# FFN2's last product: one activation table for the final norm, matmuls of a token tile ahead of the scalings, the last bank in halves, weight splits ahead of token sums

## The chip, the core and the metric

The kernel runs on one core of a Trainium2 chip. Its engines are TensorE (PE, with its weight loads shown as PEld), VectorE (DVE), ScalarE (ACT), GpSimd (POOL) and SyncE (SP). Each works through its own list of instructions in order, and they wait for each other by semaphores. The metric is the device time of one execution in microseconds, as the median of repeated runs.

## What is computed

The reference is one layer of a streaming encoder: a half-step feed-forward network (FFN1), two token mixers side by side, a second feed-forward network (FFN2), and a norm at the end. The change is in the last part:

```python
x = x + 0.5 * swiglu(rms_norm(x, ffn2_norm[l]), ffn2_w1[l], ffn2_w3[l], ffn2_w2[l])
return rms_norm(x, final_norm)

def swiglu(h, w1, w3, w2):
    return (jax.nn.silu(h @ w1) * (h @ w3)) @ w2
```

There are 512 tokens and 1024 columns, all in float32. The product of concern is the last one, `hidden @ w2`, with 22 blocks of 128 hidden rows, followed by the residual sum and the final norm of each token.

## The kernel before

**Three matmuls for one.** A float32 operand is split into a high part (rounded to the fast float32 form, a cast on ACT) and a low part (the rest, a subtraction on DVE). A product is high x high, high x low and low x high.

**Seven products for eight.** `ByTokens.run` multiplies hidden rows 0 to 15 with `w2` by a Strassen-like scheme: both operands are cut in two each way, sums of the quarters are made, and seven products of quarters take the place of eight. Rows 16 to 21 are multiplied plainly. Results are kept by tokens in eight banks X, Y, Z, W, two each, of 128 tokens x 512 columns.

- The sums of the **weights** are made by DMA: `onto` (L1893) issues on POOL's queue a DMA that adds a part of `w2` onto a buffer that holds another. The buffers are `chain` (four, tile `raw` in the trace) and `b22` (four, tile `wu`). `fetch` (L1888) loads a part plainly on SP's queue.
- The sums of the **tokens** are made on DVE from the hidden parts, in four units u, by `whole` (L1917: one operation of 1024 columns, two of 512), `s1` (L1925: one of 512 on DVE, then a cast `h0to` on ACT, then, as `rest`, another of 512 on DVE) and `s234` (L1931: three of 512).
- `prep` (L1955) splits a weight buffer: a cast of 1024 columns on ACT (`whi`, L1965) and the rest on DVE (`wlo`, through L1903). It uses three pairs of buffers in turn, so a split waits until PE is done with the piece of three splits earlier. `parts` (L1941) splits token sums in the same way.
- `seventh` (L1975) and `plainly` (L1985) are one **pass** on PE: twelve matmuls of 512 columns with one piece of weights, eight with the high part, then four with the low part. I number the passes from 0 in the order in which PE runs them: 0 to 3 go into X, 4 to 7 into Y (weights `b21`), 8 to 11 are plain passes (weights `f`), 12 to 15 go into Z, 16 to 19 into X (weights `chain` with a part added), 20 to 27 use `b22`, before and after a part is added (24 is the first after it), 28 is plain, 29 to 32 use `chain` with a third part, 33 is plain.
- `snap` (L1995) copies a pair of banks to memory on ACT. `parts`, `prep`, `snap` and all the sums are recorded by `keep`, which holds them in the order of the program text on each engine. That text is written by hand, from L2008 to L2142; it sets the order that the change alters. A DMA with no `keep` may still be moved by the scheduler.

**The end phase** (L2143 to L2174) goes over four token tiles t of 128 tokens. Each tile has two banks c of 512 columns: twelve matmuls for the first, six for the second. DVE reads a bank, scales it by half the token's norm factor and adds the residual (L2156); ACT squares the result and sums it (L2157); a small DVE operation (L2159) adds the epsilon; the reciprocal root is exp(-0.5 ln(.)) on ACT, Ln in L2160 and Exp in L2161; DVE multiplies both halves by it and by the gain `fg` (L2165), and SP stores them (L2166). In the last tile, DVE makes the product with the gain early (L2170), and ACT (L2171) and DVE (L2172) scale one half each. Before Ln and before Exp, the compiler places a load of the activation table that has the function.

Of the kernel before, what the change touches and what calls it, by code (L numbers as in the profile page):

```python
# [18 lines left out]
P = 128  # L19
# [32 lines left out]
def kernel(  # L52
# [401 lines left out]
    class Seven:  # L454
# [59 lines left out]
        def rest(s, dst, src, hi):  # L514
            keep(dve.tensor_tensor(dst, src, f32(hi), op=ALU.subtract))  # L515
# [1336 lines left out]
    class ByTokens:  # L1852
# [26 lines left out]
        def run(s, hh, hl, h, w2, hp):  # L1879
# [8 lines left out]
            def fetch(tag, k0, c):  # L1888
                to = unit(tag)
                keep(nc.sync.dma_start(to, part(k0, c)))  # L1890
                return to

            def onto(to, k0, c):  # L1893
                keep(nc.gpsimd.dma_start(to, part(k0, c), accum_op=ALU.add))
# [2 lines left out]
                return y[:, t // 2, t % 2 * P:(t % 2 + 1) * P] if len(y.shape) == 3 else y[:, t * P:(t + 1) * P]  # L1897

            def mm(ps, a, b, start=False, stop=False):
                keep(pe.matmul(ps[:], a, b, start=start, stop=stop, skip_group_check=True))  # L1900

            def two(to, a, b, op=ALU.subtract):
                keep(dve.tensor_tensor(to, a, b, op=op))  # L1903
# [21 lines left out]
            def s1(u):  # L1925
                v, to = RB[u][:, :, H:T], [h[:, 2 * u:2 * u + 2, i, H:T] for i in range(2)]
                two(v, RA[u][:, :, H:T], v)
                keep(act.copy(to[0], v))
# [20 lines left out]
            def plain_h(k0, t0):  # L1949
                return lambda k, a: [token(y[k0 + k], t0 + a) for y in (hh, hl)]  # L1950
# [4 lines left out]
            def prep(src, own=None):  # L1955
                n = made[0]
                if own:
                    hi, lo = [unit(t, F32R) for t in own]
                else:
                    made[0] += 1  # L1960
                    if n % 3 == 2:
                        hi, lo = fp.tile([P, 2, T], F32R, name="whi", tag="fg")[:], unit("E30", F32R, "wlo")
                    else:
                        hi, lo = [wp.tile([P, 2, T], F32R, tag=t, name=t, bufs=2)[:] for t in ("whi", "wlo")]
                keep(act.copy(hi, src))  # L1965
# [29 lines left out]
            def snap(ps, name, t0):  # L1995
                got = []
                for a in range(2):
                    o = xp.tile([P, T], F32, name=f"{name}{a}", tag=f"x{'hl'[a]}{dict(x0=4, up=5, m5=6)[name]}")[:]
                    keep(act.activation(o, ps[a][:], AF.Copy, scale=sc[:, t0 + a:t0 + a + 1]))
                    got.append(o)  # L2000
                return got
# [18 lines left out]
            seventh(X, plain_h(4, 0))  # L2020
            prep(b21[1])
            rest = s1(1)
            s234(1)
            rest()
            f = [fetch(tags[0], 16, 0)]
            seventh(X, plain_h(6, 0))
            prep(b21[2])
            f.append(fetch(tags[1], 16, 1))
            whole(2)
            seventh(Y, plain_h(K2, 0), True)  # L2030
            prep(b21[3])
            x0 = snap(X, "x0", 0)
            f.append(fetch(tags[2], 18, 0))
            seventh(Y, plain_h(K2 + 2, 0))
            prep(f[0])
            f.append(fetch(tags[3], 18, 1))
            seventh(Y, plain_h(K2 + 4, 0))
            prep(f[1])
            rest = s1(2)
            s234(2)  # L2040
            rest()
            seventh(Y, plain_h(K2 + 6, 0))
            prep(f[2])
            whole(3)
            plainly(16, 0, (0, 1))
            prep(f[3])
            plainly(16, 1, (2, 3), True)
            prep(chain[0])
            onto(chain[0], K2, 1)
            plainly(18, 0, (0, 1))  # L2050
            prep(chain[1])
            onto(chain[1], K2 + 2, 1)
            plainly(18, 1, (2, 3))
            prep(chain[2])
            onto(chain[2], K2 + 4, 1)
            rest = s1(3)
            seventh(Z, plain_h(0, 2), True)
            prep(chain[3])
            onto(chain[3], K2 + 6, 1)
            rest()  # L2060
            s234(3)
# [8 lines left out]
            onto(chain[1], K2 + 2, 0)  # L2070
            seventh(Z, plain_h(6, 2))
            left.append(parts(S2, 2))
            prep(chain[2])
            onto(chain[2], K2 + 4, 0)
# [4 lines left out]
            onto(chain[3], K2 + 6, 0)  # L2079
# [60 lines left out]
            residual(3)  # L2140
            for key in ((20, 0), (20, 1), (18, 0)):
                last[key] = take()  # L2142
            for t in range(NB):  # L2143
                y = ys[t]
                sums_, b_, r = [sc[:, o + t * n:o + (t + 1) * n] for o, n in ((4, 2), (12, 1), (16, 1))]
                first = 1 if t < 2 else 0
                for c in (first, 1 - first):
                    ks = [(k0, *last[k0, c], k) for k0 in (18, 20) if k0 == 20 or c == first for k in range(2)]
                    to = bank_of[t][c]
                    for k0, hi, lo, k in ks:  # L2150
                        mm(to, token(hh[k0 + k], t), hi[:, k])
                        mm(to, token(hl[k0 + k], t), hi[:, k])
                    for k0, hi, lo, k in ks:
                        mm(to, token(hh[k0 + k], t), lo[:, k], stop=(k0, k) == (20, 1))
                    v = y[:, c * T:(c + 1) * T]
                    keep(dve.scalar_tensor_tensor(v, to[:], sc[:, t:t + 1], v, op0=ALU.mult, op1=ALU.add))  # L2156
                    keep(act.activation(tmp("junk")[:], v, AF.Square, accum_out=sums_[:, c:c + 1]))  # L2157
                    if c == first:
                        keep(dve.tensor_scalar(b_, sums_[:, c:c + 1], 1.0 / D, RMS_EPS, op0=ALU.mult, op1=ALU.add))  # L2159
                keep(act.activation(r, sums_[:, 1 - first:2 - first], AF.Ln, bias=b_, scale=1.0 / D))  # L2160
                keep(act.activation(r, r, AF.Exp, scale=-0.5))  # L2161
                for c in range(2):
                    cs = slice(c * T, (c + 1) * T)
                    if t + 1 < NB:
                        keep(dve.scalar_tensor_tensor(y[:, cs], y[:, cs], r, fg[:, cs], op0=ALU.mult, op1=ALU.mult))  # L2165
                        nc.sync.dma_start(out[0, t * P:(t + 1) * P, cs], y[:, cs])  # L2166
                if t + 1 == NB:
                    g = [tmp("yg") for _ in range(2)]
                    for c in range(2):
                        keep(dve.tensor_tensor(g[c][:], y[:, c * T:(c + 1) * T], fg[:, c * T:(c + 1) * T], op=ALU.mult))  # L2170
                    keep(act.activation(g[0][:], g[0][:], AF.Copy, scale=r))  # L2171
                    keep(dve.tensor_scalar(g[1][:], g[1][:], r, None, op0=ALU.mult))  # L2172
                    for c in range(2):
                        nc.sync.dma_start(out[0, t * P:(t + 1) * P, c * T:(c + 1) * T], g[c][:])  # L2174

    tokens = ByTokens()
    ffn(nrm2, ffn2_w1, ffn2_w3, ffn2_w2, None,
# [26 lines left out]
```

## Time and profile before

| what | us |
|---|---|
| median of 3 runs | 1138.43 (1138.19 to 1140.03) |
| the profiled execution, own time | 1137.67 |
| its span on the core | 1136.0 |
| PE busy in the span | 1110.1 |
| DVE busy | 911.3 |
| ACT busy | 657.6 |
| end phase, from the first tile's first matmul to the span's end | 1099.14 to 1136.0 |

The profile is of one execution. A timeline row has the start in us from the span's beginning, the duration in us, the engine, the line of the kernel, the operation, output and inputs by the program's tile names, and shapes; where the engine had been idle, brackets give for how long and which engine's result ended it. L1900 is the helper for matmuls and L1903 the one for DVE's sums and low parts, so such rows are told apart by their tiles. A row with "x2" merges two instructions. Matmuls overlap: one lasts 0.39 us, and the next starts 0.227 us after it.

### The profile page before, as it was taken

What the parts mean: (1) busy time and instruction counts of PE and PEld (TensorE: products, weight loads), DVE (VectorE), ACT (ScalarE), POOL (GpSimd) and SP (SyncE); (2) the same over time, 40 slices, a digit from 0 to 9 for tenths busy, and PEclk for the clock granted to TensorE, in tenths of its full rate; (3) what the DMA queues carried; (4) which work ended last, traced back from release to release, by engine and by line L of the source; (5) the groups of instructions that cost most, each with busy time, mean ns of one, the idle gap of its engine ahead of it and who ended that gap; (6) DMA issues with size and microseconds to landing.
All of it is one profiled execution on the core that took longest, in us unless ns stands there. A gap on an engine that the chain in (4) does not pass through costs nothing. (4 is left out here: it accounts for less than half of the span.)

```text
span 1136.0 us, 19524 instructions
## 1 busy us (share of the span) xinstructions
PE 1110.1 (98%) x7640; PEld 974.5 (86%) x7640; DVE 911.3 (80%) x1427; ACT 657.6 (58%) x1090; POOL 106.3 (9%) x170
## 2 busy tenths in 40 slices
PE   9999999999999999999999999999999999999992
PEld 7899999988887888887777777888999999978782
DVE  6889999977566888677776668779988999989563
ACT  6645665543346755355878767536666566645545
POOL 2000000010000112311000010130000000012200
PEclk9999999999999999999999999999999999999996
DMA  8433333354434434355113236633344333377941
GB/s 260 135 93 107 99 112 106 100 176 121 121 108 112 109 98 116 101 142 139 38 39 110 66 109 205 185 93 93 112 139 121 113 96 109 113 204 162 209 167 74
DMA packets 198074, 139.55 MB, mean 123 GB/s; under 512 B 10558, under 2 KB 178558, under 8 KB 197982
## 3 DMA queue, kind: packets, MB, share of 16 engines
q1 hardware_dynamic: 185710, 110.77, 33.3%
q0 software_dynamic: 10032, 26.74, 9.1%
q8 instruction: 60, 0.98, 0.4%
q10 hardware_dynamic: 2240, 0.79, 0.3%
q14 instruction: 32, 0.26, 0.1%
HBM read 123.41 MB, written 14.88 MB: 122 GB/s over the span
## 5 line engine op out<-in xcount | busy, mean ns | idle before, releaser
L133 ACT CAST whi<-raw 128x1024 fp32r<-128x1024 f32 (+2 forms) x93 | 90.0, 969 | 103.3 <-issue 16.6
L134 DVE TENSOR_TENSOR wlo<-raw,whi 128x1024 fp32r<-128x1024 f32 (+2 forms) x93 | 104.3, 1122 | 22.4 <-ACT whi L133 22.1
L142 PE MATMUL zc<-xh,wlo 128*128 128x256 f32 x296 | 83.7, 283 | 0.0
L142 PE MATMUL zc<-xl,whi 128*128 128x256 f32 x296 | 83.7, 283 | 0.0
L142 PE MATMUL zc<-xh,whi 128*128 128x256 f32 x296 | 83.7, 283 | 0.0
L142 PE MATMUL za<-e,wtwo 128*128 128x256 f32 x480 | 64.2, 283 | 0.0
L142 PEld LDWEIGHTS za<-e,wtwo 128*128 128x128 f32 x480 | 59.6, 188 | 0.0
L512 ACT CAST wtwo<-wsum 128x1024 fp32r<-128x1024 f32 x37 | 38.9, 1052 | 31.1 <-PE za L142 31.1
L142 PEld LDWEIGHTS zc<-xh,wlo 128*128 128x128 f32 x296 | 56.7, 191 | 0.0
L142 PEld LDWEIGHTS zc<-xl,whi 128*128 128x128 f32 x296 | 56.7, 191 | 0.0
L142 PEld LDWEIGHTS zc<-xh,whi 128*128 128x128 f32 x296 | 56.6, 191 | 0.0
L142 PE MATMUL pgt<-xh,whi 128*128 128x512 f32 x128 | 53.0, 414 | 0.0
L515 DVE TENSOR_TENSOR wlo<-raw,whi 128x1024 fp32r<-128x1024 f32 x41 | 49.9, 1218 | 2.5 <-ACT whi L512 2.5
L524 DVE TENSOR_TENSOR wsum<-wsum,raw 128x512 f32<-128x512 f32 x74 | 50.9, 688 | 1.2
L524 DVE TENSOR_TENSOR wsum<-raw 128x512 f32<-128x512 f32 x74 | 50.5, 683 | 0.0
L142 PE MATMUL pgt<-xh,wlo 128*128 128x512 f32 x128 | 50.1, 391 | 0.0
L142 PE MATMUL pgt<-xl,whi 128*128 128x512 f32 x128 | 50.0, 391 | 0.0
L512 ACT CAST whi<-wsum 128x1024 fp32r<-128x1024 f32 x37 | 38.8, 1048 | 16.7 <-PE zc L142 13.4
L512 ACT CAST whi<-raw 128x1024 fp32r<-128x1024 f32 x41 | 43.1, 1051 | 8.9 <-PE zc L142 7.9
L598 ACT ACTIVATE fs<-fa 128x512 f32<-128x512 f32 x39 | 24.7, 633 | 38.8 <-DVE fa L631 31.5
L515 DVE TENSOR_TENSOR wtwo<-wsum,wtwo 128x1024 fp32r<-128x1024 f32 x37 | 45.1, 1218 | 0.0
L515 DVE TENSOR_TENSOR wlo<-wsum,whi 128x1024 fp32r<-128x1024 f32 x37 | 45.0, 1217 | 0.0
(693 smaller groups left out, 3612.4 us busy)
## 6 DMA issues: line engine op xcount, KB each, us to landing
raw<-in_ffn_w_dram SPq DMA_DIRECT2D x106, 512.0 KB
raw<-in_w_in_dram SPq DMA_DIRECT2D x40, 512.0 KB
wu<-in_ffn_w_dram SPq DMA_DIRECT2D x18, 512.0 KB
raw<-in_ffn_w_dram POOLq DMA_DIRECT2D x12, 512.0 KB, 8.8
raw<-in_w_out_dram SPq DMA_DIRECT2D x8, 512.0 KB
raw<-in_ffn_w_dram SPq DMA_DIRECT2D x8, 384.0 KB
gsave<-gs SPq DMA_DIRECT2D x9, 256.0 KB
xin<-in_x_dram SPq DMA_DIRECT2D x4, 512.0 KB
```

The lines of the kernel that those rows point to most:

```text
L133: marks["wide"] = act.copy(hi[:], raw[:])
L134: marks["rest"] = (eng or dve).tensor_tensor(lo[:], raw[:], hi[:].bitcast(F32), op=ALU.subtract)
L142: mm = pe.matmul(ps, w, x_, start=first and n == 0, stop=last and n == 2, skip_group_check=chain)
L512: keep(act.copy(dst, src))
L515: keep(dve.tensor_tensor(dst, src, f32(hi), op=ALU.subtract))
L524: keep(dve.tensor_tensor(to, a, b, op=ALU.add))
L598: keep(act.activation(sa[:], a_[:], AF.Silu))
```

## The change

Four edits, all in `ByTokens.run`:

1. **One table.** `preload_act_table_set("natural_log_exp_and_others")` stands ahead of the end phase.
2. **Scalings later.** The two scalings and stores of a tile become a function `finish(t)`. For tiles 0 and 1 it is called one tile later, after that tile's second bank has been read and squared; for tile 2 it is called between the two banks of tile 3.
3. **The last bank in halves.** Tile 3's second bank is multiplied, read, squared and at the end scaled in two halves of 256 columns; its first half's gain product is made early, the other two pieces are scaled in one operation each. There are three last stores for two.
4. **Weights ahead of sums.** In the hand-written order, `prep` of a pass's weights moves up by about one pass, ahead of `s1` or between `s1` and `s234`, with the fetches that follow it; the four `onto(chain[u], K2 + 2 * u, 0)` move from behind their `prep`s to behind the last `onto` of `b22`.

```diff
             onto(chain[3], 6, 1)
+            prep(b21[0])
             rest = s1(0)
+            seventh(X, plain_h(2, 0))
+            prep(b21[1])
+            f = [fetch(tags[0], 16, 0)]
             s234(0)
             rest()
-            seventh(X, plain_h(2, 0))
-            prep(b21[0])
-            whole(1)
             seventh(X, plain_h(4, 0))
-            prep(b21[1])
+            prep(b21[2])
+            f.append(fetch(tags[1], 16, 1))
+            whole(1)
+            seventh(X, plain_h(6, 0))
+            prep(b21[3])
+            f.append(fetch(tags[2], 18, 0))
             rest = s1(1)
+            x0 = snap(X, "x0", 0)
+            seventh(Y, plain_h(K2, 0), True)
+            prep(f[0])
+            f.append(fetch(tags[3], 18, 1))
             s234(1)
             rest()
...
             prep(chain[0])
-            onto(chain[0], K2, 0)
...
             onto(b22[3], 6, 1)
+            for u in range(NU):
+                onto(chain[u], K2 + 2 * u, 0)
...
+            keep(act.preload_act_table_set("natural_log_exp_and_others"))
+
+            def finish(t):
+                y, r = ys[t], sc[:, 20 + t:21 + t]
+                for c in range(2):
+                    cs = slice(c * T, (c + 1) * T)
+                    keep(dve.scalar_tensor_tensor(y[:, cs], y[:, cs], r, fg[:, cs], op0=ALU.mult, op1=ALU.mult))
+                    nc.sync.dma_start(out[0, t * P:(t + 1) * P, cs], y[:, cs])
...
+                    if t + 1 == NB and c != first:
+                        finish(t - 1)
+                        g = tmp("yg")
+                        keep(dve.tensor_tensor(g[:], y[:, 0:T], fg[:, 0:T], op=ALU.mult))
+                    pieces = [slice(0, T)] if c == first or t + 1 < NB else [slice(0, H), slice(H, T)]
+                    for cols in pieces:
...
+                if 0 < t < NB - 1:
+                    finish(t - 1)
+                keep(act.activation(r, q, AF.Ln, bias=b_, scale=1.0 / D))
                 keep(act.activation(r, r, AF.Exp, scale=-0.5))
...
+            keep(act.activation(g[:], g[:], AF.Copy, scale=r))
+            nc.sync.dma_start(out[0, t * P:(t + 1) * P, 0:T], g[:])
+            for cols in (slice(T, T + H), slice(T + H, D)):
+                keep(dve.scalar_tensor_tensor(y[:, cols], y[:, cols], r, fg[:, cols], op0=ALU.mult, op1=ALU.mult))
+                nc.sync.dma_start(out[0, t * P:(t + 1) * P, cols], y[:, cols])
```

On DVE, where the first unit's token sums stand: `rb<-ra,rb` is `s1`, the rows with `s_` are `s234`, `wlo<-raw` is the low part of pass 3's weights and `wlo<-wu` that of passes 4 and 5.

```order
 L1903 TENSOR_TENSOR rb<-hh_9405,hl_9406 128x512
 L1903 TENSOR_TENSOR wlo<-raw,whi 128x1024
+L1903 TENSOR_TENSOR wlo<-wu,whi 128x1024
 L1903 TENSOR_TENSOR rb<-ra,rb 128x2x256
+L1903 TENSOR_TENSOR wlo<-wu,whi 128x1024
 L1903 TENSOR_TENSOR s_10841<-rb,ra 128x512
 L1903 TENSOR_TENSOR s_10843<-ra 128x512
```

One weights' low part now stands ahead of `s1`, and another between `s1` and `s234`.

On ACT at the same place and on to the second unit: `h0to` is the cast inside `s1`, `x_` are the snaps of X.

```order
 L1965 CAST whi<-raw 128x1024 x2
+L1965 CAST whi<-wu 128x1024
 L1928 CAST h0to_8201<-rb 128x2x256
-L1965 CAST whi<-wu 128x1024 x2
+L1965 CAST whi<-wu 128x1024 x3
 L1928 CAST h0to_8201<-rb 128x2x256
-L1965 CAST whi<-wu 128x1024 x2
-L1999 ACTIVATE x_10976<-tx_10833,small 128x512
-L1999 ACTIVATE x_10978<-tx_10834,small 128x512
```

One of the casts of weights has moved ahead of the first `h0to`; each of the later ones that DVE takes next after an `s1` stands behind that unit's `h0to`.

On DVE in the end phase, from the second token tile's first bank to the fourth's: L2169 is the reading of a bank, L2172 the small operation, L2147 the scaling. This is the order after:

```order
L2169 SCALAR_TENSOR_TENSOR yt<-tz_10838,small,yt 128x512
L2172 TENSOR_SCALAR small<-small 128x1
L2169 SCALAR_TENSOR_TENSOR yt<-ty_10836,small,yt 128x512
L2147 SCALAR_TENSOR_TENSOR yt<-yt,small,fgain 128x512 x2
L2169 SCALAR_TENSOR_TENSOR yt<-tx_10833,small,yt 128x512
L2172 TENSOR_SCALAR small<-small 128x1
L2169 SCALAR_TENSOR_TENSOR yt<-tw_10839,small,yt 128x512
L2147 SCALAR_TENSOR_TENSOR yt<-yt,small,fgain 128x512 x2
L2169 SCALAR_TENSOR_TENSOR yt<-tx_10834,small,yt 128x512
```

Before, the same rows stood there with two scalings behind each tile's second reading; now the scalings behind a tile's second reading are those of the tile before it.

More of the change, by code (lines that the diff above doesn't have):

```diff
@@ L1899, in mm @@
             def mm(ps, a, b, start=False, stop=False):
-                keep(pe.matmul(ps[:], a, b, start=start, stop=stop, skip_group_check=True))
+                keep(pe.matmul(ps if isinstance(ps, bass.AP) else ps[:], a, b, start=start, stop=stop, skip_group_check=True))
             def two(to, a, b, op=ALU.subtract):
@@ L2022, in run @@
+            prep(b21[3])
+            f.append(fetch(tags[2], 18, 0))
             rest = s1(1)
+            x0 = snap(X, "x0", 0)
+            seventh(Y, plain_h(K2, 0), True)
+            prep(f[0])
+            f.append(fetch(tags[3], 18, 1))
             s234(1)
             rest()
[L2025 to L2028, printed above, removed]
+            seventh(Y, plain_h(K2 + 2, 0))
+            prep(f[1])
@@ L2029, in run @@
             whole(2)
[L2030 to L2036, printed above, removed]
             seventh(Y, plain_h(K2 + 4, 0))
-            prep(f[1])
+            prep(f[2])
             rest = s1(2)
+            seventh(Y, plain_h(K2 + 6, 0))
+            prep(f[3])
             s234(2)
             rest()
-            seventh(Y, plain_h(K2 + 6, 0))
@@ L2043, in run @@
-            prep(f[2])
-            whole(3)
             plainly(16, 0, (0, 1))
-            prep(f[3])
-            plainly(16, 1, (2, 3), True)
             prep(chain[0])
             onto(chain[0], K2, 1)
-            plainly(18, 0, (0, 1))
+            whole(3)
+            plainly(16, 1, (2, 3), True)
             prep(chain[1])
             onto(chain[1], K2 + 2, 1)
-            plainly(18, 1, (2, 3))
+            rest = s1(3)
+            plainly(18, 0, (0, 1))
             prep(chain[2])
@@ L2149, in run @@
                     to = bank_of[t][c]
[L2150 to L2174, printed above, removed]
+                    if t + 1 == NB and c != first:
+                        finish(t - 1)
+                        g = tmp("yg")
+                        keep(dve.tensor_tensor(g[:], y[:, 0:T], fg[:, 0:T], op=ALU.mult))
@@ new lines, in run @@
+                    pieces = [slice(0, T)] if c == first or t + 1 < NB else [slice(0, H), slice(H, T)]
+                    for cols in pieces:
+                        for k0, hi, lo, k in ks:
+                            mm(to[:, cols], token(hh[k0 + k], t), hi[:, k, cols])
+                            mm(to[:, cols], token(hl[k0 + k], t), hi[:, k, cols])
+                        for k0, hi, lo, k in ks:
+                            mm(to[:, cols], token(hh[k0 + k], t), lo[:, k, cols], stop=(k0, k) == (20, 1))
+                        v, q = y[:, c * T + cols.start:c * T + cols.stop], sc[:, 4 + 3 * t + n:5 + 3 * t + n]
+                        keep(dve.scalar_tensor_tensor(v, to[:, cols], sc[:, t:t + 1], v, op0=ALU.mult, op1=ALU.add))
+                        keep(act.activation(tmp("junk")[:, cols], v, AF.Square, accum_out=q))
+                        if n == 0:
+                            keep(dve.tensor_scalar(b_, q, 1.0 / D, RMS_EPS, op0=ALU.mult, op1=ALU.add))
+                        elif cols.stop < T:
+                            keep(dve.scalar_tensor_tensor(b_, q, 1.0 / D, b_, op0=ALU.mult, op1=ALU.add))
+                        n += 1
```

17 lines of the change are left out of this document (7 added, 10 removed).

## Prediction

> **What bounds the kernel now.** I read the page first, then its last two windows, then the timelines of PE, ACT, DVE and SP in the end phase, and last those of DVE, ACT and PE where the token sums are made.
>
> ```profile
> PE 1110.1 (98%) x7640; PEld 974.5 (86%) x7640; DVE 911.3 (80%) x1427; ACT 657.6 (58%) x1090; POOL 106.3 (9%) x170
> 1060.00:1100.00 40.00, 38.05 (x168) 31.19 (x167) 24.94 (x27) 19.92 (x23) 3.68 (x4) 1.00 0.79 205
> 1100.00:1137.00 37.00, 15.62 (x69) 12.58 (x68) 14.59 (x25) 18.77 (x33) 0.00 (x0) 0.75 0.15 57
> ```
>
> PE is busy for 98% of the span, so elsewhere only PE's waits can be won. The last window (columns: PE, PEld, DVE, ACT, POOL, granted clock, DMA share, GB/s) is different: PE works 15.6 of 37 us. PE's part of the end phase:
>
> ```profile
> 1099.14 0.39 PE L1900 MATMUL tz<-wu,hh 128*128 128x512 f32 x1
> 1101.86 0.39 PE L1900 MATMUL ty<-whi,xh 128*128 128x512 f32 x1
> 1103.22 0.39 PE L1900 MATMUL tz<-wu,hh 128*128 128x512 f32 x1
> 1115.23 0.39 PE L1900 MATMUL tw<-wlo,hh 128*128 128x512 f32 x1
> ```
>
> Call S = 1099.14 the start of the first token tile. Twelve matmuls take 2.72 us (0.2266 each), a tile's eighteen 4.08, and PE is through at 1115.62, 20.4 us before the span's end at 1136.0. What runs after it is a chain of ACT and DVE:
>
> ```profile
> 1102.69 0.74 DVE L2156 SCALAR_TENSOR_TENSOR yt<-tz,small,yt 128x512 f32<-128x512 f32 x1
> 1104.22 0.15 DVE L2159 TENSOR_SCALAR small<-small 128x1 f32<-128x1 f32 x1 [0.79 <-ACT junk L2157]
> 1104.29 0.74 DVE L2156 SCALAR_TENSOR_TENSOR yt<-ty,small,yt 128x512 f32<-128x512 f32 x1
> 1105.06 0.63 ACT L2157 ACTIVATE junk<-yt 128x512 f32<-128x512 f32 x1 [0.88 <-DVE yt L2156]
> 1105.60 0.19 ACT L2157 ACTIVATION_READ_ACCUMULATOR junk<-yt 128x1 f32 x1
> 1105.80 1.28 ACT L2160 ACT_TABLE_LOAD   x1
> 1107.10 0.29 ACT L2160 ACTIVATE small<-small 128x1 f32<-128x1 f32 x1
> 1107.41 1.28 ACT L2161 ACT_TABLE_LOAD   x1
> 1108.70 0.20 ACT L2161 ACTIVATE small<-small 128x1 f32<-128x1 f32 x1
> 1108.94 1.42 DVE L2165 SCALAR_TENSOR_TENSOR yt<-yt,small,fgain 128x512 f32<-128x512 f32 x2 [3.91 <-ACT small L2161]
> 1110.27 0.75 DVE L2156 SCALAR_TENSOR_TENSOR yt<-tz,small,yt 128x512 f32<-128x512 f32 x1
> 1132.22 0.81 SPq L2174 DMA_DIRECT2D out_dram<-yg  x2
> ```
>
> A tile costs 7.58 us (1102.69 to 1110.27) where PE needs 4.08. DVE waits 3.91 us for the square root's two halves, of which two table loads are 2.56, and the next tile's reading of its bank stands behind that wait. So the end phase is bound by this chain.
>
> **Part one: the end phase.** The loads inside the loop go (eight of 1.28, 10.2 us, all on the chain), and one is placed behind the last weights' cast, hidden by PE's first tile: ACT has nothing to do there until the first Square. Ln starts at 1107.10, 0.02 us after its load ended at 1107.08, so a load's row is its whole price. The Trainium skill (ScalarE: Activation LUTs, "What ACT_TABLE_LOAD costs") puts a switch of sets at 1283 ns and a drain of about 1380 behind it; by that the eight would be worth 21.3 us, 11.1 more than by the row, and the trace has no place for them.
>
> Two scalings (L2165) now stand behind the next tile's two bank readings, so they no longer hold PE's banks' reading up. DVE per middle tile: a reading 0.74, the wait and the small op to the second reading 0.86, that one 0.67, scalings 1.34: 3.6 us, below PE's 4.08. PE therefore becomes the bound of the first three tiles, and the last tile follows PE. From S, in us:
>
> - tile 3's first bank: PE ends at 3 x 4.08 + 2.88 = 15.12; reading to 15.89, Square with its read to 16.65, small op 16.75;
> - then DVE has tile 2's two scalings (1.34, to 18.09) and the early gain product:
>
> ```profile
> 1127.72 1.28 DVE L2170 TENSOR_TENSOR yg<-yt,fgain 128x512 f32<-128x512 f32 x2
> 982.45 0.42 DVE L635 SCALAR_TENSOR_TENSOR fh<-za,fs 128x256 f32<-128x256 f32 x1
> 992.78 0.37 ACT L512 COPY fa<-za 128x256 f32<-128x256 f32 x1
> ```
>
> - product 0.60, to 18.69. The last bank's halves are in by then: PE ends at 16.7, or 18.1 if each 256-column matmul cost as much as a 512-column one; either way before 18.69, so halving costs PE nothing that counts;
> - half a reading, 0.41 by the row with 256 columns, to 19.10; half a Square. No row shows it: between 0.37 (the 256-column copy without a read) and 0.73 (the whole one with its read). I take 0.47, the copy with the part of the read that sticks out (0.10 here). Then small op, second half's reading from 19.70 to 20.11, Square to 20.61, Ln 20.91, Exp 21.14;
> - half a scaling, 0.41, to 21.55; SP issues the first output at 21.6, two more 0.43 behind each other.
>
> Before, SP's first of two issues stood at 1132.22 = S + 33.1, and the span ended 3.8 later. Now 21.6 + 3.8, plus 0.43 for a third issue, minus some 0.35 for a last transfer of half the size: 25.5 against 36.9. Part one is worth -11.4 us. Bounds: halved Squares 0.26 longer each, +0.5; if they and the middle steps run without my gaps, -0.7.
>
> **Part two: weights ahead of the token sums.** A pass is twelve matmuls with one split piece of weights; three buffers hold pieces. Before, DVE is the engine that PE waits for:
>
> ```profile
> 1008.36 1.22 DVE L1903 TENSOR_TENSOR wlo<-raw,whi 128x1024 fp32r<-128x1024 f32 x1
> 1009.50 0.68 DVE L1903 TENSOR_TENSOR rb<-ra,rb 128x512 f32<-128x512 f32 x1
> 1010.22 0.62 ACT L1928 CAST h0to<-rb 128x512 fp32r<-128x512 f32 x1 [4.64 <-DVE rb L1903]
> 1010.74 2.00 ACT L1965 CAST whi<-wu 128x1024 fp32r<-128x1024 f32 x2
> 1020.38 1.26 ACT L1999 ACTIVATE x<-tx,small 128x512 f32<-128x512 f32 x2
> 1012.08 0.39 PE L1900 MATMUL ty<-whi,hh 128*128 128x512 f32 x1
> 1026.15 0.39 PE L1900 MATMUL ty<-whi,hh 128*128 128x512 f32 x1
> 1040.88 1.23 DVE L1903 TENSOR_TENSOR wlo<-raw,whi 128x1024 fp32r<-128x1024 f32 x1 [1.64 <-ACT whi L1965]
> ```
>
> Passes 4 to 7 take 14.07 us (1012.08 to 1026.15) for 4 x 2.72 = 10.88: PE loses 3.2 there and nothing until 1071. DVE's first idle time is the 1.64 before 1040.88. The order now puts a weights' low part right behind each first sum s1. But its high part is cast on ACT, in order behind `h0to`, which waits for that s1. So DVE stands still for 0.53 (`h0to`) + 1.05 (cast) + two handovers = 1.7 us, in the second unit 2.9, as the two snaps (L1999, 1.2) lie between too. Four units: 8.1 us of DVE idle that wasn't there, on the engine that is short.
>
> Step by step with DVE at 1.14 (1024 columns) and 0.60 (512), everything to 1009.50 unchanged: low parts of passes 4 to 7 end at 1010.6, 1014.1, 1017.7 and 1021.1; due are 1013.9, 1016.6, 1019.3, 1022.1, so the loss of 3.2 goes. Then s1 of unit 1 ends at 1021.8, `h0to` 1022.4, snaps 1023.6, cast 1024.7: pass 8, due at 1012.08 + 10.88 = 1022.96, starts 1.75 late. Its low part ends 1025.9, unit 1's other sums 1028.2, low part of pass 9 1029.5 (due 1029.35), unit 2's whole sums 1031.7, low part of 10 1032.95 (due 1032.35: 0.6 late), s1 1033.55, `h0to`, cast 1035.2: pass 11 is 1.2 late. Unit 3 repeats it on passes 13 and 14: 0.6 and 1.2. With three waits of 0.15, and 0.11 to refill PE after each of the eight (a matmul behind a wait takes 0.50, not 0.39, as the row at 1071.79 below), PE loses 6.7 where it lost 3.2: +3.5 us. From pass 16 on no sums are left. The fetches of `f` move up on SP with the low parts that free their buffers; the first is issued at 1010.7 and needed at 1023.6, so they cost nothing, and with SP twice as slow still nothing.
>
> **Part three: the accumulating DMAs.** PE's last wait:
>
> ```profile
> 1068.77 1.07 PE L1900 MATMUL tz<-wlo,xh 128*128 128x512 f32 x4
> 1071.79 0.50 PE L1900 MATMUL tx<-whi,sph 128*128 128x512 f32 x1 [1.95 <-ACT whi L1965]
> 1036.52 1.17 POOL L1894 DMA_DIRECT2D raw<-in_ffn_w_dram  x1 [25.47 <-DVE wlo L1903]
> 1042.57 1.06 ACT L1965 CAST whi<-raw 128x1024 fp32r<-128x1024 f32 x1 [1.20 <-DMA raw<-in_ffn_w_dram]
> 1048.51 1.05 ACT L1965 CAST whi<-raw 128x1024 fp32r<-128x1024 f32 x1 [0.98 <-DMA raw<-in_ffn_w_dram]
> 1053.48 1.05 ACT L1965 CAST whi<-raw 128x1024 fp32r<-128x1024 f32 x1 [2.03 <-DMA raw<-in_ffn_w_dram]
> 1057.83 1.19 POOL L1894 DMA_DIRECT2D wu<-in_ffn_w_dram  x1 [0.54 <-DVE wlo L1903]
> 1070.69 1.04 ACT L1965 CAST whi<-wu 128x1024 fp32r<-128x1024 f32 x1 [5.63 <-DMA wu<-in_ffn_w_dram]
> 1073.20 1.05 ACT L1965 CAST whi<-wu 128x1024 fp32r<-128x1024 f32 x1 [0.94 <-DMA wu<-in_ffn_w_dram]
> ```
>
> Pass 24 was due at 1069.68 and starts at 1071.79; with the refill 2.2 us are lost. Its piece, issued on POOL at 1057.83, lands at 1070.6, behind four accumulations into `chain` that are issued earlier and needed later. They land one by one, 2.5 us apart (1070.69, 1073.20), 5.0 where plain fetches share the engines (1048.51 to 1053.48); an idle queue takes 6.0 (1036.52 to 1042.57). Now `b22` goes first: its first piece is split some 4.5 us later (1062.5), finds the queue empty, lands at 1068.5, and pass 24 is due 1073.3, its cast 1.05 before: the 2.2 go. The four `chain` pieces follow 2.5 apart, 1078.7 to 1086.4; passes 29 to 32 begin at 1086.9 and each 2.72 later: 7 us of room. On POOL only the gain's load stands behind them. Pass 19's piece is near: issued at 1050.5 (after pass 15's low part) it lands at 1058 to 1059 and its cast must start by 1058.6: 0 to 0.5, taken as 0.
>
> **The sum.** -11.4 + 3.5 - 2.2 = -10.1 us. The profiled execution took 1137.67 (its span 1136.0), so 1127.6; it lies 0.8 below the median of 1138.43, so 1128.3 for the median. A change under 0.2% (2.3 us) counts as none.
>
> **The rivals.**
>
> - A: ACT's and DVE's queues give enough slack that no pass waits in the sums at all. For it: before, DVE's order alone made PE wait. Against: the cast's place behind `h0to` in ACT's row. Then -11.4 - 3.2 - 2.2 = -16.8: 1121.6. Chance 0.08.
> - B: a new DMA wait as large as the old one comes at pass 18, 19 or 24, since the accumulations now start 3.5 us later and the fetches fall among them. For it: 5.0 us between landings when shared. Then +2.2: 1130.5. Chance 0.12.
> - C, slower: eight accumulations now stand in one row on POOL's queue, the first landing at 1068.5. At d us each the last lands at 1068.5 + 7d, and pass 32 needs it by 1094. At 2.5 there is room; above 3.6 PE is late by 7d - 25.5, which eats the 10.1 at d = 5.09. At 5.5, a little over the slowest pair seen (5.0), PE is 13.0 late: +2.9, 1141.3. Against: between 1062 and pass 28 no plain fetch runs beside them. Chance 0.04, half of it near enough to 5.09 to show no change.
>
> **How the numbers follow.** My forecast, part two as stepped, gets 0.76: 1128.3, of itself 1126 to 1130.3 (tail -0.7 to +0.5, a pass's wait off by 1, the runs' own spread). The range 1124.8 to 1131.2 takes in B and leaves out A and C. The forecast, A and B are all faster: 0.96. C gives 0.02 for no change and 0.02 for slower.
>
> **What would show it.** In the profile after: one table load in the end phase; DVE's steps of the middle tiles 4.08 apart; SP's first of the last three issues 21.6 after S; DVE idle 1.7, 2.9, 1.7, 1.7 with ACT named; PE waits at passes 8, 11 and 14; none near pass 24. If PE waits for nothing between passes 4 and 16, or S comes earlier than 1099.14, part two is wrong; if DVE, not PE, sets the middle tiles, part one is.

## Result, and the profile after

| | before | after |
|---|---|---|
| median of 4 runs | 1138.38 us | 1130.72 us (1130.57 to 1131.88) |
| the profiled execution, its span | 1137.67, 1136.0 | 1130.77, 1129.1 |
| first matmul of the stage (`tx<-whi,h0to`) | 1001.17 | 1001.18 |
| S, the start of the first token tile | 1099.14 | 1102.15 |
| from that first matmul to S | 97.97 | 100.97 |
| end phase, S to the span's end | 36.8 | 26.9 |

The ratio is 0.9932, with a 95% interval of 0.9915 to 0.9949: 7.7 us faster, where 10.1 were predicted. Up to 1001 us nothing has moved. In the profile the end phase is 9.9 us shorter (forecast 11.4), and the stretch ahead of it 3.0 us longer (forecast 1.3).

First the waits of PE from 1000 us on, in the kernel after. The columns are the total, how often, and the longest.

```profile
PE tw L1900 <- DVE yt L2169: 3.4, 1, 3.4
PE ty L1900 <- ACT whi L1965: 1.5, 1, 1.5
PE tx L1900 <- ACT whi L1965: 1.5, 1, 1.5
PE tz L1900 <- ACT whi L1965: 1.0, 1, 1.0
PE tw L1900 <- ACT whi L1965: 1.0, 1, 1.0
PE tz L1900 <- DVE wlo L1903: 0.5, 1, 0.5
PE ty L1900 <- DVE wlo L1903: 0.4, 1, 0.4
```

Five of these are the waits that part two forecast: `ty` 1.5 (pass 8) and 0.4 (pass 10), `tw` 1.0 (pass 11), `tz` 0.5 and 1.0 (passes 13 and 14). No row stands near pass 24. Two rows weren't in the sum: `tx`, 1.5 us, which is pass 19, and `tw`, 3.4 us, which is the last bank of the end phase. The timeline of PE shows the three largest waits with their places:

```profile
1012.09 0.39 PE L1900 MATMUL ty<-whi,hh 128*128 128x512 f32 x1
1024.62 0.50 PE L1900 MATMUL ty<-whi,hh 128*128 128x512 f32 x1 [1.49 <-ACT whi L1965]
1061.19 0.50 PE L1900 MATMUL tx<-whi,xh 128*128 128x512 f32 x1 [1.45 <-ACT whi L1965]
1102.15 0.39 PE L1900 MATMUL tz<-wu,hh 128*128 128x512 f32 x1
1117.70 0.28 PE L1900 MATMUL tw<-wlo,hh 128*128 128x256 f32 x1
1121.37 0.58 PE L1900 MATMUL tw<-whi,xh 128*128 128x256 f32 x1 [3.40 <-DVE yt L2169]
1122.61 0.41 PE L1900 MATMUL tw<-wlo,hh 128*128 128x256 f32 x1
```

Pass 4 starts at 1012.09; fifteen passes of 2.72 later pass 19 is due at 1052.89, and it starts at 1061.19. Of these 8.30 us, 1.61 are its own wait: the 1.45 of the row, which counts idle time only from the end of the matmul before, and 0.16 because that one lasts 0.39 where the next was due after 0.227. So the token sums cost 6.7 (forecast 6.7), and pass 19, with the 0.11 to refill PE, costs 1.7. The last bank's first half is done at 1117.98; its second half doesn't start before 1121.37. DVE at the same places, the four idle times in the sums first, then the end phase:

```profile
1012.97 1.22 DVE L1903 TENSOR_TENSOR wlo<-wu,whi 128x1024 fp32r<-128x1024 f32 x1 [1.64 <-ACT whi L1965]
1024.60 1.23 DVE L1903 TENSOR_TENSOR wlo<-wu,whi 128x1024 fp32r<-128x1024 f32 x1 [2.78 <-ACT whi L1965]
1035.08 1.23 DVE L1903 TENSOR_TENSOR wlo<-wu,whi 128x1024 fp32r<-128x1024 f32 x1 [1.63 <-ACT whi L1965]
1045.55 1.22 DVE L1903 TENSOR_TENSOR wlo<-raw,whi 128x1024 fp32r<-128x1024 f32 x1 [1.63 <-ACT whi L1965]
...
1109.15 0.75 DVE L2169 SCALAR_TENSOR_TENSOR yt<-tz,small,yt 128x512 f32<-128x512 f32 x1 [1.10 <-PE tz L1900]
1113.23 0.75 DVE L2169 SCALAR_TENSOR_TENSOR yt<-tx,small,yt 128x512 f32<-128x512 f32 x1 [0.41 <-PE tx L1900]
1117.31 0.75 DVE L2169 SCALAR_TENSOR_TENSOR yt<-tx,small,yt 128x512 f32<-128x512 f32 x1 [0.40 <-PE tx L1900]
1118.92 1.41 DVE L2147 SCALAR_TENSOR_TENSOR yt<-yt,small,fgain 128x512 f32<-128x512 f32 x2
1120.24 0.69 DVE L2160 TENSOR_TENSOR yg<-yt,fgain 128x512 f32<-128x512 f32 x1
1120.84 0.48 DVE L2169 SCALAR_TENSOR_TENSOR yt<-tw,small,yt 128x256 f32<-128x256 f32 x1
1123.06 0.48 DVE L2169 SCALAR_TENSOR_TENSOR yt<-tw,small,yt 128x256 f32<-128x256 f32 x1 [1.01 <-PE tw L1900]
1124.68 0.88 DVE L2183 SCALAR_TENSOR_TENSOR yt<-yt,small,fgain 128x256 f32<-128x256 f32 x2 [1.14 <-ACT small L2179]
```

The tiles' first readings stand 4.08 apart, each behind PE: PE sets the pace, as forecast. The first half of the last bank is read at 1120.84, S + 18.69, to the hundredth the forecast. But PE begins the second half of this bank only when that reading is through, and DVE then waits for PE. The second reading is at S + 20.91 instead of S + 19.70. SP's first of the last three issues follows at S + 23.04 instead of S + 21.6:

```profile
1125.19 0.33 SPq L2184 DMA_DIRECT2D out_dram<-yt  x1
```

The windows (columns: length, then busy time of PE, PEld, DVE, ACT, POOL, then granted clock, DMA share, GB/s) show that the second half is also slow:

```profile
1102.00:1118.00 16.00, 15.98 (x74) 13.16 (x72) 11.72 (x20) 7.62 (x20) 0.00 (x0) 1.00 0.14 55
1118.00:1121.00 3.00, 0.00 (x0) 0.00 (x0) 2.21 (x6) 0.72 (x2) 0.00 (x0) 1.00 0.31 122
1121.00:1123.00 2.00, 1.63 (x6) 1.35 (x6) 0.48 (x2) 0.51 (x2) 0.00 (x0) 0.51 0.45 173
```

After 3.4 us of standing still PE has a granted clock of 0.51. The six matmuls from 1121.37 to 1123.02 take 1.65 us.

### The profile page after: what moved, and what is told of

It is laid out like the page before. It is cut to its first block, busy times and chain, and to the rows that moved or that the text cites. A ratio compares the mean times of both kernels' runs of the same rounds, so it can differ in the third digit from the quotient of the medians.

```text
span 1129.1 us, 19528 instructions
## 1 busy us (share of the span) xinstructions
PE 1112.0 (98%) x7646; PEld 975.0 (86%) x7646; DVE 911.1 (81%) x1429; ACT 648.5 (57%) x1085; POOL 106.1 (9%) x170
## 4 chain that ended last, share of the span: by engine, by line
PE 92%; issue 4%; DVE 1%; DMA 1%; ACT 1%; POOL 0%; DVEq 0%; POOLq 0%; ACTq 0%
PE za L142 23%; PE zc L142 14%; PE pgt L142 8%; PE pd L142 6%; PE pk L142 6%; PE ppj L1702 4%; PE pw L142 4%; PE pq L142 4%; PE tx L1900 3%; PE pa L142 3%; PE pb L142 3%; PE pv L142 2%; PE tz L1900 2%; PE pl L142 1%; DMA raw<-in_ffn_w_dram 1%
## 5 line engine op out<-in xcount | busy, mean ns | idle before, releaser
L512 ACT CAST whi<-wsum 128x1024 fp32r<-128x1024 f32 x37 | 38.8, 1048 | 16.7 <-PE zc L142 13.4
```

What stands on the lines that cost most here:

```text
L512: keep(act.copy(dst, src))
```

## The experiments

The theory after the result: two things are missing from the sum. First, PE may not write one half of a bank while DVE still has to read the other half, so the halves are a chain (about 1.5 us). Second, an accumulating DMA for pass 19 lands late because plain fetches share the DMA engines with it (about 1.7 us). Its rivals were that part two's waits were too small in the sum, or that part one's chain was mis-sized elsewhere. All times below are medians; each stands beside a run of the kernel before on the same chip. This table is read from the timelines of PE:

| run | median, beside before | ratio, 95% interval | first matmul | to S | end phase |
|---|---|---|---|---|---|
| e1_tail_only | 1126.88, 1137.70 | 0.9904 (0.9889 to 0.9919) | 1001.65 | 96.94 | 26.2 |
| e2_front_only | 1141.15, 1137.70 | 1.0033 (1.0023 to 1.0043) | 1001.34 | 100.97 | 36.8 |
| e3_onto_only | 1135.9, 1137.70 | 0.9984 (0.9975 to 0.9993) | 1001.51 | 95.78 | 36.8 |
| e4_bank_whole | 1129.66, 1137.70 | 0.9926 (0.9909 to 0.9942) | 1001.44 | 101.62 | 25.2 |
| e5_casts_first | 1123.37, 1138.43 | 0.9865 (0.9849 to 0.9882) | 1001.59 | 93.97 | 26.9 |
| e6_late_early | 1129.98, 1138.43 | 0.9929 (0.9915 to 0.9944) | 1002.15 | 101.85 | 26.9 |
| e7_swap | 1130.03, 1138.43 | 0.9928 (0.9913 to 0.9942) | 1002.41 | 101.04 | 25.2 |
| e8_late_mid | 1129.49, 1137.45 | 0.9927 (0.9912 to 0.9942) | 1001.13 | 99.69 | 26.2 |
| e9_best_late | 1121.54, 1137.45 | 0.9863 (0.9846 to 0.9879) | 1001.25 | 93.27 | 25.1 |
| e10_best | 1122.06, 1137.45 | 0.9863 (0.9849 to 0.9878) | 1001.33 | 93.76 | 25.1 |

The stage's first matmul moves by up to 1.3 us from run to run with nothing changed ahead of it, so edits worth 1 or 2 us are read from the two columns behind it, not from the median.

### The end phase alone

The kernel after, with the order of the passes and sums as before:

```diff
-            prep(b21[0])
             rest = s1(0)
-            seventh(X, plain_h(2, 0))
-            prep(b21[1])
-            f = [fetch(tags[0], 16, 0)]
             s234(0)
             rest()
+            seventh(X, plain_h(2, 0))
+            prep(b21[0])
+            whole(1)
...
```

> The order of the token sums as before, the end phase as after. Theory 1 (the new order ahead of the end phase costs 3.0 us: the end phase begins at 1102.15 after and 1099.14 before; the end phase gives 9.9, 36.9 down to 26.95): the end phase begins at 1099.1 as before, PE's wait of 2.2 us at pass 24 is back, the waits at passes 8, 11, 14 and 19 are gone, the time is 9.9 us under before, about 1128.5. Rival (the new order gains, and the end phase gives less than it seems): slower than 1130.7.

It is 10.8 us faster than before: part one alone is worth more than the whole change. The bank's wait is there in the same size, but the second half ran at the full clock. PE, then the window, whose mean of 0.94 is that low only because it goes on for 1.2 us past the last matmul (from 1117 to 1119 us the clock is 1.00):

```profile
1117.81 0.39 PE L1900 MATMUL tw<-whi,xh 128*128 128x256 f32 x1 [3.39 <-DVE yt L2171]
1118.51 0.28 PE L1900 MATMUL tw<-wlo,hh 128*128 128x256 f32 x1
```

```profile
1117.00:1120.00 3.00, 0.98 (x6) 0.78 (x6) 1.40 (x4) 1.13 (x5) 0.00 (x0) 0.94 0.44 170
```

From 1117.81 to 1118.79 the six matmuls take 0.98 us, 0.67 less than in the kernel after, and the end phase is shorter by the same 0.7. One thing was not expected: with the old order PE's wait at pass 24 was due to be back in full, but it is 0.84 us where it was 1.95 before, and the stretch to S is 1.0 us shorter than before. The fourth accumulation into `chain` is cast 51.2 us behind the stage's first matmul here and 52.3 before, in the same order. No run shows why, so some 1.0 of the gain is not the end phase's.

### The order alone

The reverse: the kernel after with the end phase as before.

```diff
-            keep(act.preload_act_table_set("natural_log_exp_and_others"))
-            def finish(t):
...
-                    pieces = [slice(0, T)] if c == first or t + 1 < NB else [slice(0, H), slice(H, T)]
-                    for cols in pieces:
...
+                for c in range(2):
+                    cs = slice(c * T, (c + 1) * T)
+                    if t + 1 < NB:
```

> The order of the token sums and of the accumulating DMAs as after, the end phase as before. Theory 1: the end phase begins at 1102.15 and lasts 36.9, the time is 3.0 us over before, about 1141.4. Rival: the order by itself gains 2 us or more, 1136.4 or less.

The two reorderings together make the kernel 3.45 us slower. To S it takes 100.97 us, the kernel after's number to the hundredth, and the waits are the same seven less the bank's. With e1's -10.8 this gives -7.4, beside -7.7 measured for the whole change. By the two columns the parts add up less well, to -8.6 beside -6.9: 1.0 of the difference is pass 24 in e1, and 0.7 its full clock in the last half.

### The accumulating DMAs alone

The kernel before, with this edit:

```diff
             prep(chain[0])
-            onto(chain[0], K2, 0)
...
             onto(b22[3], 6, 1)
+            for u in range(NU):
+                onto(chain[u], K2 + 2 * u, 0)
```

> Before, with the one move of the four accumulations into chain behind those into b22. Theory: PE's wait at pass 24 (2.2 us) goes, since the piece lands some 8 us earlier, nothing else moves, 1136.2. Rival (the DMA engines are full there, so the wait only moves to passes 29 to 32): no change, 1138.4.

To S it is 2.19 us shorter, the 2.2 of the forecast; the median gives 1.8. All that is left of PE's waits is this:

```profile
PE ty L1900 <- ACT whi L1965: 1.0, 1, 1.0
PE ty L1900 <- DVE wlo L1903: 0.9, 2, 0.5
```

These are passes 5 to 7; neither pass 24 nor pass 19 waits. So pass 19's wait isn't a price of this move. Part two alone is then e2 less e3: 100.97 - 95.78 = 5.2 us slower, of which 3.5 were forecast and the rest is pass 19.

### The last bank in one piece

```diff
-                    pieces = [slice(0, T)] if c == first or t + 1 < NB else [slice(0, H), slice(H, T)]
+                    pieces = [slice(0, T)]
```

> After, with the last bank multiplied, read and squared in one piece. Theory 2 (PE's second half waits 3.4 us for DVE to read the first half of the same bank, and DVE reads it only after two scalings and a product; then PE runs at half clock): without halves DVE reads the bank at once at 1120.8 by the times of after, Square, Ln and Exp end at 1122.9 in place of 1124.6, so 1.7 us less than after, 1129.0, and the granted clock stays at 1.00 to the last matmul. Rival (the half's wait is hidden behind DVE's other work): the time is that of after or 0.5 over it, as the longer Square comes last.

```profile
1121.75 0.74 DVE L2169 SCALAR_TENSOR_TENSOR yt<-tw,small,yt 128x512 f32<-128x512 f32 x1
1123.85 0.88 DVE L2183 SCALAR_TENSOR_TENSOR yt<-yt,small,fgain 128x256 f32<-128x256 f32 x2 [1.35 <-ACT small L2179]
```

S is at 1103.06 here. The whole bank is read from S + 18.69, in one step of 0.74, and the last scaling starts at S + 20.79, where the halves have S + 22.53. The end phase is 1.74 us shorter, and PE has no wait in it. So the halving, ordered as it is, saves nothing but costs 1.7 us. The profiled execution is only 0.8 below the kernel after's (the median 1.1), because the stage began 0.3 later and pass 19 waits 2.0 us in this run, not 1.5.

### Casts ahead of the sums

In the sums ACT's queue stands still behind `h0to`, and DVE behind ACT. Here the cast of the next weights is issued ahead of each first sum `s1`, the low part where it was:

```diff
+                if later:
+                    wide.append((hi, lo))
+                    return lambda: two(lo, src, f32(hi))
...
+            low = prep(b21[1], later=True)
             rest = s1(0)
             seventh(X, plain_h(2, 0))
-            prep(b21[1])
+            low()
```

and the same for `f[0]`, `f[3]` and `chain[2]` ahead of `s1(1)`, `s1(2)` and `s1(3)`.

> After, with four casts of weights (pieces of passes 5, 8, 11 and 14) placed ahead of s1 on ACT, so that they no longer stand behind h0to; DVE's order is unchanged. Theory 3 (DVE's four idle times of 1.6, 2.8, 1.6 and 1.6 us come from the cast's place behind h0to): they go, PE's waits at passes 8, 10, 11, 13 and 14 go (6.7 us with the refills), a wait at pass 19 of 1.5 to 3 stays, the end phase begins at 1095.5 to 1097, the time is 5 to 6.5 us under after, 1124 to 1126. Rival (DVE has too much work in this stretch, wherever the casts stand, or the three buffers hold the casts back): under 2 us.

ACT and DVE at the first unit, and then the waits of PE:

```profile
1009.07 1.06 ACT L1965 CAST whi<-wu 128x1024 fp32r<-128x1024 f32 x1 [1.66 <-PE tx L1900]
1011.77 0.62 ACT L1928 CAST h0to<-rb 128x512 fp32r<-128x512 f32 x1 [1.65 <-DVE rb L1903]
```

```profile
1011.06 0.68 DVE L1903 TENSOR_TENSOR rb<-ra,rb 128x512 f32<-128x512 f32 x1
1011.66 1.22 DVE L1903 TENSOR_TENSOR wlo<-wu,whi 128x1024 fp32r<-128x1024 f32 x1
```

```profile
PE tw L1900 <- DVE yt L2176: 3.4, 1, 3.4
PE tx L1900 <- ACT whi L1965: 1.1, 1, 1.1
```

The cast is done before `h0to` begins, and DVE goes from the first sum (`rb`) straight to the low part, where it had stood still for 1.64 us. All five waits in the sums are gone. To S it takes 93.97 us, 7.0 less than the kernel after and 4.0 less than before. This shows the cause of what the sums cost: the place of one cast in ACT's queue, four times. Pass 19's wait stays, at 1.1 us.

### The fetches that lie beside pass 19's piece

The two fetches of `late` were moved ahead of those of `b22`, so that they would run while the DMA engines are idle and only 1 MB would be left beside the accumulations:

```diff
+            late = [fetch("E20", 16, 1), fetch("E21", 16, 0)]
             b22 = [fetch(t, K2 + 2 * u, 1) for u, t in enumerate(("E10", "E11", "E00", "E01"))]
...
-            late = [fetch("E20", 16, 1), fetch("E21", 16, 0)]
```

> After, with the two fetches of the pieces of passes 28 and 33 issued ahead of those of b22 on SP, so that they move while the DMA engines are idle. Theory 4 (pass 19's piece lands 1.6 us late because 2 MB of plain fetches go ahead of it): only 1 MB is left, it lands before 1058.5, PE's wait at pass 19 goes, 1.6 us under after, 1129.1. Rival (the accumulations are late by their own issue, 8 us later than before): the wait stays, 1130.7.

The wait did not go: PE waits twice, at passes 18 and 19, 2.0 us in all. The edit did more than was meant: the fetches of `late` wait for buffers and are issued at 1033.84 and 1037.30, and the first two of `b22` were now queued behind them, so 1.8 MB still moved beside the four accumulations (2.1 in the kernel after), part of it beside earlier ones. It tells nothing for or against the cause.

A cleaner one: `late` between the second and the third of `b22`, so that about 1 MB less falls beside the fourth accumulation.

```diff
-            b22 = [fetch(t, K2 + 2 * u, 1) for u, t in enumerate(("E10", "E11", "E00", "E01"))]
+            b22 = [fetch(t, K2 + 2 * u, 1) for u, t in enumerate(("E10", "E11"))]
+            late = [fetch("E20", 16, 1), fetch("E21", 16, 0)]
+            b22 += [fetch(t, K2 + 4 + 2 * u, 1) for u, t in enumerate(("E00", "E01"))]
...
-            late = [fetch("E20", 16, 1), fetch("E21", 16, 0)]
```

> After, with the two fetches of the pieces of passes 28 and 33 issued behind the first two fetches of b22 and ahead of the other two, which wait longest: the first two of b22 stay where they are after, 1 MB moves while the DMA engines are idle, and 1 MB is left beside the fourth accumulation into chain. Theory 4 (plain fetches take the engines ahead of the accumulation: 7.4 us between its landing and the one before with 2 MB beside it, 5.4 with 1 MB, 2.5 to 3.3 with none): it lands about 5.4 us behind the third, near 1058, and PE's wait at pass 19 shrinks from 1.6 to 0 or a few tenths; no wait at pass 18. Rival (late by its own issue): the wait stays at 1.6.

The DMA queues of this kernel from 1053 to 1060 us, when the fourth accumulation is under way (packets, MB, share of the 16 engines; `software_dynamic` is POOL's queue, which issues the accumulations, `hardware_dynamic` is SP's). The kernel after first, then this one, and behind each the casts on ACT that take the third and fourth accumulated piece:

```profile
q1 hardware_dynamic: 821, 1.58, 64.4%
q0 software_dynamic: 272, 0.52, 40.8%
```

```profile
1052.76 1.05 ACT L1965 CAST whi<-raw 128x1024 fp32r<-128x1024 f32 x1 [1.62 <-DVE xl L1903]
1060.10 1.04 ACT L1965 CAST whi<-raw 128x1024 fp32r<-128x1024 f32 x1 [4.62 <-DMA raw<-in_ffn_w_dram]
```

```profile
q0 software_dynamic: 272, 0.52, 41.8%
q1 hardware_dynamic: 385, 0.72, 32.3%
```

```profile
1052.80 1.05 ACT L1965 CAST whi<-raw 128x1024 fp32r<-128x1024 f32 x1 [1.51 <-DMA raw<-in_ffn_w_dram]
1058.74 1.05 ACT L1965 CAST whi<-raw 128x1024 fp32r<-128x1024 f32 x1 [3.22 <-DMA raw<-in_ffn_w_dram]
```

With 0.72 MB of fetches instead of 1.58 beside the same 0.52 MB, the fourth piece can be cast at 1058.74 instead of 1060.10, and PE's waits list no `tx` row any more. To S it is 1.28 us shorter. The accumulation was issued at the same place, 1050.58 here and 1050.61 in the kernel after, so its issue is not what made it late. Four kernels with the order of the kernel after have a wait of 1.45 to 2.03 us at pass 19, so the gain is clear of their spread, though it rests on one profiled execution. So the fetches beside it are shown as the cause of most of pass 19's wait. By the median alone (ratio 0.9927 beside 0.9932) this couldn't be told from the kernel after.

### The first half read earlier

The scalings of tile 2 and the gain product move behind the reading of the last bank's first half, so that PE is released earlier:

```diff
-                    if t + 1 == NB and c != first:
-                        finish(t - 1)
-                        g = tmp("yg")
-                        keep(dve.tensor_tensor(g[:], y[:, 0:T], fg[:, 0:T], op=ALU.mult))
...
+                        if cols.stop < T:
+                            finish(t - 1)
+                            g = tmp("yg")
+                            keep(dve.tensor_tensor(g[:], y[:, 0:T], fg[:, 0:T], op=ALU.mult))
```

> After, with tile 2's two scalings and the gain product behind the reading of the last bank's first half on DVE, halves kept. Theory 2: DVE reads the first half at 1118.9 by the times of after, PE's second half begins at 1119.4 at full clock, the second reading starts at 1121.3 in place of 1123.1: 1.7 us under after, 1129.0. Rival: as after, 1130.7.

```profile
1120.22 0.47 DVE L2165 SCALAR_TENSOR_TENSOR yt<-tw,small,yt 128x256 f32<-128x256 f32 x1
1120.61 1.41 DVE L2147 SCALAR_TENSOR_TENSOR yt<-yt,small,fgain 128x512 f32<-128x512 f32 x2
1122.61 0.48 DVE L2165 SCALAR_TENSOR_TENSOR yt<-tw,small,yt 128x256 f32<-128x256 f32 x1
```

S is at 1103.45 here, so the first half is read at S + 16.77 instead of 18.69. PE's wait falls from 3.4 to 1.5 us, and while it multiplies, DVE does the scalings. The end phase is 1.75 us shorter, as much as with one whole bank. Halves that are released early bring just what one piece brings, then; halves that aren't cost 1.75. In the profiled execution the stage began 1.2 us later than in the kernel after, so that one is only 0.45 shorter; the median shows 0.7.

### The parts put together

The casts ahead and the first half read earlier (e10_best), and these two with the fetches' order of e8 (e9_best_late):

```diff
+            low = prep(b21[1], later=True)
             rest = s1(0)
...
+                        if cols.stop < T:
+                            finish(t - 1)
```

> Three edits on top of after: the four casts ahead of s1, the two fetches ahead of the last two of b22, and tile 2's scalings behind the first half's reading. Theories 2 to 4 together: no waits of PE in the token sums (6.7 us with refills), none or 1 at pass 19 (1.6), an end phase of 25.2 in place of 26.9: 9 to 10 us under after, 1121 to 1122. Rival (the gains overlap): no better than the casts alone, 1123.4.

> The four casts ahead of s1 and tile 2's scalings behind the first half's reading, on top of after; the fetches as after. Theories 2 and 3: 1.7 us under the kernel with the casts alone (1123.4), 1121.7, with the wait of 1.3 at pass 19 as there.

Both beat both kernels: some 16 us under before (ratio 0.9863 each), some 9 under the kernel after. All that e9_best_late has left of PE's waits, and its first and last matmul behind the bank's wait:

```profile
PE tw L1900 <- DVE yt L2173: 1.5, 1, 1.5
PE tx L1900 <- ACT whi L1965: 0.4, 1, 0.4
```

```profile
1111.82 0.39 PE L1900 MATMUL tw<-whi,xh 128*128 128x256 f32 x1 [1.47 <-DVE yt L2173]
1112.52 0.28 PE L1900 MATMUL tw<-wlo,hh 128*128 128x256 f32 x1
```

After a wait of 1.47 us the half takes 0.98 us, from 1111.82 to 1112.80, at the full clock. Pass 19 waits 0.4 us here and 0.9 in e10_best, which has more fetches beside its fourth accumulation (1.40 MB for 1.05 from 1042.7 to 1052.4 us); the medians, 0.5 us apart, don't tell the two apart.

## Why the prediction came out as it did

It was right in the sign and inside its range, 1124.8 to 1131.2, but outside the 1126 to 1130.3 that the likeliest case had for itself. By its steps:

- **Loads and scalings (part one): right.** One table load is left. PE sets the tiles at 4.08, and the first half of the last bank is read at the forecast S + 18.69. No run has the one without the other, so what each is worth alone stays open.
- **"Halving costs PE nothing that counts": wrong** and it is the whole of the tail's miss, 1.45 us. The step asked when PE would have finished both halves if it ran on, and never whether it might. PE's second half waits for DVE's reading of the first, which is of the same tile and bank; e4 and e7 show the price, 1.75 us, of which the low clock behind the long wait is 0.7 (e1). The tail came out at -9.9, not -11.4. The Trainium skill (PSUM — Partial Sum Buffer, "PSUM bank collisions raise a hardware error") asks for exactly this wait: two engines may not be in the same partitions of one bank at once, even at different columns, so the guard goes by bank. The trace agrees, with 3.40 us of waiting for a reading of other columns; no run here let the two overlap, and none tells a guard by bank from one by tile. The prediction hadn't drawn on it.
- **Token sums (part two): right**, with its mechanism and its size. DVE's idle times were forecast as 1.7, 2.9, 1.7, 1.7 (their sum is 8.0, not the 8.1 that it names) and are 1.64, 2.78, 1.63, 1.63; pass 8 starts at 1024.62 for 1024.7, pass 11 at 1035.10 for 1035.2; its three waits of 0.15, too short for a row of their own, are starts 0.12 to 0.14 late (1029.43, 1039.90, 1050.37); the sums cost 6.7 for 6.7. e5 takes the cast out of its place, and all of it goes.
- **Pass 24 (part three): right.** The wait is gone; e3 alone gains 2.19 for 2.2.
- **Pass 19, "0 to 0.5, taken as 0": wrong.** It waits 1.45 us by its row, and costs 1.7. The step lets the piece land at 1058 to 1059 and doesn't say from what; its one price for a landing beside fetches is 5.0 us behind the piece before, from a pair of before that had 1.02 MB of fetches beside it (1048 to 1054 us):

```profile
q1 hardware_dynamic: 525, 1.02, 48.8%
```

  Here 1.58 MB lay beside it, and the two casts stand 7.3 us apart (1052.76 and 1060.10). What would lie beside it in the new order was not counted. Its issue time was right, 1050.61 for 1050.5.

The sum again with the two mis-sized terms: -10.1 + 1.5 + 1.7 = -6.9, and the two profiled executions differ by 6.9. The medians differ by 0.8 us more, since the profiled run of before was 0.7 under its median and that of after wasn't. So of the rivals B came nearest, at 1130.5: a new DMA wait at one of the three passes that it named, of 1.7 us rather than 2.2. It has only half of what was missing, and not the tail's 1.5, so that its time lies 0.2 us from the measured one is luck. A's condition did not hold in this kernel; e5 shows what it takes. C's did not either: neither pass 29 nor any of 30 to 32 has a wait.

One thing stays open: why the fourth accumulation comes at different times in kernels with the same order up to there. Pass 19's wait is 1.45 us in e2_front_only and the kernel after, 1.48 in e7_swap and 2.03 in e4_bank_whole; pass 24's was 1.95 before and is 0.84 in e1_tail_only.

## What to carry to other kernels

Before a bank's work is cut into halves for overlap, ask who is let into the bank while the other half is unread: if the guard goes by bank, the cut is a chain and not a pipeline. Where weights are moved ahead of sums, look for what stands in front of their cast in its own engine's queue: here the cast, and not the sum, held DVE up, and moving it too turned +5.2 us into a gain. When a transfer's margin is under a microsecond, count the megabytes that will lie beside it in the new order, not those that lay beside it in the old one.

## What the runs showed of the hardware

- **PE's clock behind a wait.** In five kernels PE waits 3.39 or 3.40 us ahead of its last six matmuls. In three (the kernel after, e5_casts_first, e6_late_early) the granted clock was 0.50 to 0.51 by then, the six took 1.65 us, and the end phase 26.9. In e1_tail_only and e8_late_mid it was still 1.00, they took 0.98 us, and the end phase 26.2. In the three the clock fell 3.1, 2.3 and 1.9 us after the matmul ahead of the wait, so the length of the wait doesn't decide. The Trainium skill (TensorE: Matmul & The Clock Gate, "Part 1: The HAM clock gate") describes a window of about 3.4 us that runs freely, whatever the kernel does, and a clock that is halved after an idle one. The traces agree with the window: in the twelve of this case the full clock lasts 1109.33, 1112.75, 1116.16 or 1119.57 us, which are steps of 3.41. They don't ask for an idle one: counted back from the fall in steps of 3.41 us, PE was busy by its rows for at most 0.43 of the last window and for at least 0.47 of every one before it. By that, as an estimate, some 1.95 us of idle time inside one window (0.57 of 3.41) are enough, and fewer than 1.8 (0.53) are not; the waits of 1.47 us in e7_swap, e9_best_late and e10_best never brought it down while matmuls were left.
- **Accumulating DMAs beside plain ones.** Accumulations of 0.5 MB land 2.5 us apart alone, 5.9 with 0.72 MB of fetches beside them and 7.3 with 1.58 MB, by the casts behind them (1052.80 to 1058.74 and 1052.76 to 1060.10). The bytes alone don't set it: with 1.02 MB it was 5.0 before and 3.9 in e1_tail_only (1048.96 to 1052.87). What sets the engines' sharing wasn't tried.
